# Down-projection passes with four seven-product pairs instead of two, and loads queued in unit order

## The chip, the cores and the metric

The kernel runs on one core of one Trainium2 chip. The metric is the device time of one execution in microseconds (us); lower is better. Several executions of each kernel are timed and their median is given, and one further execution is recorded by the hardware profiler. The engines are TensorE (PE, matrix products), VectorE (DVE), ScalarE (ACT), GpSimd (POOL) and SyncE (SP); the last issues most of the loads, and 16 DMA engines move the data.

## The reference, cut to what matters

One layer of a hybrid block on 256 tokens of width 2048, in float32: a normalised input projection, attention beside a convolution, an output projection, and then a SwiGLU feed-forward part of hidden width 5632. Only that last part is touched:

```python
hn = rms_norm(h, norm2_g[l])
a  = einsum('bsd,df->bsf', hn, w_gate[l])          # 256x2048 . 2048x5632
bu = einsum('bsd,df->bsf', hn, w_up[l])
h  = h + einsum('bsf,fd->bsd', silu(a) * bu, w_down[l])   # 256x5632 . 5632x2048
```

## The kernel before, in words

**Precision.** A float32 product is made of three matmuls in a reduced float32 format: each operand is split into a rounded part, "hi", and a residue, "lo", and hi·hi, lo·hi and hi·lo are added up in PSUM. So each weight tile that is loaded (`raw`, or `wb` for a pair) is rounded by ACT (`whi`, `wh`), and its residue (`wlo`, `wlt`, `wlb`) is found by a subtraction. The subtraction runs on DVE, or, where `by_dma` is set, ACT writes the negated raw tile and a DMA issued by POOL adds the raw tile to it (`round_chunk`, L320 to L324; the split on DVE is L329).

**The feed-forward part** works on hidden blocks of 512 columns. Blocks 0 to 10 lie in three groups of 4, 4 and 3 (`FGROUPS`). For each block, gate and up products are formed, multiplied and transposed (`transposed`, L831 to L842) into activations; after each group, `down_pass` multiplies the group's activations with the rows of `w_down` that belong to them. There are two passes for each group, each over 1024 output columns, in two halves of 512. A group of four blocks has 16 k-tiles of 128 rows; its two passes are called long passes here.

**Units.** The work is cut into units, listed in the order in which PE takes them (`ORDER`, `DORDERS`):

- A "two" (kind `g` or `u`, `multiply_two`) takes two k-tiles for one column half: 12 matmuls of 128x512. `g` is the first half and `u` the second.
- A "pair" (kind `s`, `multiply_pair`) takes two k-tiles for both column halves at once, by a scheme with seven products of block sums instead of eight: 21 matmuls, where four halves of twos would take 24. Its weights are combined by three operations on DVE (`round_pair`, L966 to L968), rounded by ACT (L969, L972) and split by DVE (`split_pair`, L975, L976). The activations need sums of their own, "forms", made by `make_down_forms` in small steps while the group's third and fourth blocks run.

In a long pass before the change, 2 of the 8 pairs of k-tiles go through pairs and the others through twos: the orders are `gguuggsguugsuu` and `sgggugggusuuuu`, 2 pairs and 12 twos each. All residues of these passes are found on DVE. A gate/up block has 4 pairs and 8 twos in the order `sggsggsuusuu`, and four of its twos have their residue made by DMA (two of them in the first block after a down pass).

**Order of the engines' queues.** No scheduler reorders anything: `run_chunks` writes out all instructions. When it is at unit t, it first writes the splits of units up to t+2, then loads, then the rounding of units up to t+3, and then unit t's matmuls. Each engine runs its own list in order and waits where a buffer or an operand isn't there yet. Loads of pairs are written six units ahead (`PAIR_AHEAD`), loads of twos three units ahead, at their rounding; both go through SP's queue, which stands still while its next load waits for a buffer. There are 5 buffers for `raw`, 2 for `wb`, 3 each for `whi` and `wlo`, 2 for `wh`, `wlt` and `wlb`, and 1 for `wt`. When the last unit with sums ends, `bank_sums` (L1092 to L1099) empties six PSUM banks, and `down_whole` (L1154) the other two; the next pass needs the same banks.

Of the kernel before, what the change touches and what calls it, by code (L numbers as in the profile page):

```python
# [12 lines left out]
F32 = mybir.dt.float32  # L13
F32R = mybir.dt.float32r
AF = mybir.ActivationFunctionType
# [70 lines left out]


HD = N // P
ND = 2
DORDERS = {4: ("gguuggsguugsuu", "sgggugggusuuuu"), 3: ("gguusggsuu", "gggsgsuuuu")}  # L90

Q1, Q6, Q7, Q5, Q2, Q4, Q3, QX = range(8)

# [2 lines left out]

HI_AHEAD, LO_AHEAD = 3, 2

PAIR_AHEAD = 6

FIRSTS = [sum(FGROUPS[: g + 1]) for g in range(len(FGROUPS))]

# [20 lines left out]
def tile_block(  # L123
# [117 lines left out]
    def start(gen):  # L241
        running.append(gen)
# [98 lines left out]
    def multiply(c):  # L341
# [42 lines left out]
        if c["done"]:  # L384
            start(c["done"](ps))

    def run_chunks():
        n = len(chunks)
        i = j = p = 0
        behind = [k for k in range(n) if chunks[k].get("kind") == "s"][NS]  # L390
        for t in range(n):
            hi_lead, lo_lead = lead(t)
            while j < min(i, t + 1 + lo_lead):
                chunks[j]["split"](chunks[j])
                j += 1
            while p < min(n, t + 1 + PAIR_AHEAD):
                if chunks[p].get("kind") == "s":

                    if p < behind and p > t + hi_lead:
                        break  # L400
                    load_pair(chunks[p])
                p += 1
            while i < min(n, t + 1 + hi_lead):
                if i in before:
                    before[i]()
                chunks[i]["load"](chunks[i])
                chunks[i]["round"](chunks[i])
# [413 lines left out]
    def transposed(j, aa):  # L821
        last = j + 1 in FIRSTS
        b = j - group_of(j)[1]
        for t in range(N // P // 2):

            pool_, tag = (acc_ps, "acc") if last else (aux_ps, "aux")
            pt = pool_.tile([P, 2, S], F32, tag=tag, name="ps_a")
            for i in range(2):
                for m in range(NM):
                    c = (2 * t + i) * P  # L830
                    pe.transpose(pt[:, i, m * P : (m + 1) * P], aa[m][:, c : c + P], ident)  # L831
# [10 lines left out]
            dve.tensor_tensor(lo, pt, hi.bitcast(F32), ALU.subtract)  # L842
# [14 lines left out]

    def make_down_forms(g):

        fp = ffn["pool"]  # L860
        gap = lambda: lag(5 if FGROUPS[g] == 4 else 2)
        a11, a21 = (raw_act[0][:, :, m * P : (m + 1) * P] for m in range(NM))
        a12, a22 = (raw_act[1][:, :, m * P : (m + 1) * P] for m in range(NM))

        hi = fp.tile([P, 7, ND, P], F32R, tag="dhi", name="dhi")
        lo = fp.tile([P, 3, ND, P], F32R, tag="dlo", name="dlo")
        fa, fb = (lhs.tile([P, 2, ND, P], F32, tag=t, name="dsums") for t in ("lhi", "llo"))
        act.copy(hi[:, 0], a11)
        dve.scalar_tensor_tensor(fa[:, 0], a21, -1.0, a22, ALU.mult, ALU.subtract)
        yield from gap()  # L870
        act.copy(hi[:, 1], a12)
        dve.scalar_tensor_tensor(fa[:, 1], fa[:, 0], -1.0, a11, ALU.mult, ALU.subtract)
        yield from gap()
        act.activation(hi[:, 2], a22, AF.Copy, scale=-1.0)
        dve.tensor_tensor(fb[:, 0], a11, a21, ALU.subtract)
        yield from gap()
        act.copy(hi[:, 3:5], fa)
        dve.tensor_tensor(fb[:, 1], a12, fa[:, 1], ALU.subtract)
        yield from gap()
        act.copy(hi[:, 5:7], fb)  # L880
        for i, a in ((0, a11), (1, a12)):
            dve.tensor_tensor(lo[:, i], a, hi[:, i].bitcast(F32), ALU.subtract)
            yield from gap()
        dve.scalar_tensor_tensor(lo[:, 2], a22, -1.0, hi[:, 2].bitcast(F32), ALU.mult, ALU.subtract)
        yield from gap()
        pairs = [lhs.tile([P, 2, ND, P], F32R, tag=t, name="dlo2") for t in ("lhi", "llo")]
        for i, f in ((0, fa), (1, fb)):
            dve.tensor_tensor(pairs[i], f, hi[:, 3 + 2 * i : 5 + 2 * i].bitcast(F32), ALU.subtract)
            yield from gap()
        los = [lo[:, 0], lo[:, 1], lo[:, 2], pairs[0][:, 0], pairs[0][:, 1], pairs[1][:, 0], pairs[1][:, 1]]  # L890
        down_forms[g] = {f: (hi[:, i], los[i]) for i, f in enumerate((0, 1, 3, 4, 5, 6, 2))}

    forms = {}
# [56 lines left out]
    def load_pair(c):  # L952
        c["b"] = early.tile([P, 4, N], F32, tag="wb", name="wb")
        for i, kind in enumerate("ug"):
            w, col = c["from"][kind]
            sp.dma_start(out=c["b"][:, 2 * i : 2 * i + 2, :],
                         in_=w.rearrange("(k p) n -> p k n", p=P)[:, c["rows"], col : col + N])
# [82 lines left out]
    def fast_block(order, pairs, twos, sources, operands, half, whole, by_dma=dict(g=(), u=())):  # L1040

        units, sums = [], {}
        left = dict(s=list(pairs), g=list(twos), u=list(twos))
        for kind in order:
            what = left[kind].pop(0)
            c = dict(kind=kind, sums=sums, done=None, first={}, last={}, rows=what["rows"], **operands)
            if kind == "s":
                c.update(p=what["p"], load=lambda c: None, round=round_pair, split=split_pair, multiply=multiply_pair,
                         uses=[q for q, _, _ in PRODUCTS])
# [12 lines left out]
        units[-1].update(done=whole, prompt=True)  # L1062
        chunks.extend(units)
# [8 lines left out]

    def down_pass(g, j0, nb):
        k0 = j0 * HD
        ks = [k for k in range(nb * HD) if k >= 2 * HD or k % HD >= ND]
        twos = [dict(ks=(k0 + a, k0 + b), rows=slice(k0 + a, k0 + b + 1, b - a), k=None)
                for a, b in zip(ks[::2], ks[1::2])]
        for i, order in enumerate(DORDERS[nb]):
            n = 2 * i
            end = {}  # L1080
            fast_block(order, [dict(p=p, rows=slice(k0 + p, k0 + p + HD + 1, HD)) for p in range(ND)], twos,
                       dict(g=(w_down, n * N), u=(w_down, (n + 1) * N)),
                       dict(pairs=lambda: down_forms.get(g), plain=actT.get),
                       lambda sums, n=n, end=end: down_half(g, n, sums, end),
                       lambda sums, n=n, end=end: down_whole(g, n, sums, end))

    halfway = {}

# [158 lines left out]
```

## Time and profile before

| | |
|---|---|
| Time, median of 3 runs | 1048.26 us (1048.14 to 1048.77) |
| Time of the profiled execution | 1048.92 us |
| Its span in the trace | 1047.1 us |
| PE busy | 1036.2 us, 4663 matmuls in the record |
| DVE busy | 900.6 us |
| ACT busy | 621.6 us |
| Clock granted to PE | full speed from the start |

A time in the profile is a time from the span's start. A matmul's recorded length overlaps the next one's, so the distance between starts tells what a matmul costs. "Idle before" in an engine's list is followed by what ended the wait. The long passes of the first group run from about 517 to 602 us, those of the second from about 769 to 854 us.

### The profile page before, as it was taken

To read this page: it belongs to the slowest core of one execution; us is meant where nothing else is said; L and a number is where in the kernel's file an instruction comes from. 1 tells how busy PE (TensorE), PEld (TensorE's weight loads), DVE (VectorE), ACT (ScalarE), POOL (GpSimd) and SP (SyncE) were. 2 spreads that over 40 slices of the span, in tenths; PEclk is the share of its full clock that TensorE was granted. 3 is DMA by queue.
4 is the path that set the end of the run, shared out by engine and by line. 5 is a ranking of instruction groups with operands and counts; after the bars stand their busy time and mean duration, and the time that the engine had idled before them with its cause. 6 is when DMAs were issued, how large, how long until landed. Compare 5 with 4: busy or idle time off the path is not lost.

```text
span 1047.1 us, 12933 instructions
## 1 busy us (share of the span) xinstructions
PE 1036.2 (99%) x4663; PEld 852.5 (81%) x4663; DVE 900.6 (86%) x1095; ACT 621.6 (59%) x786; POOL 100.5 (10%) x143
## 2 busy tenths in 40 slices
PE   9999999999999999999999999999999999999998
PEld 7888887877788788888888888888888888888886
DVE  7899889898765599999787898999878789989897
ACT  7544666755756565776463657666644446657442
POOL 0130122201100100000001010000000110000010
PEclk9999999999999999999999999999999999999999
DMA  9657654453546566987867789879757879798683
GB/s 335 227 182 280 212 163 167 154 181 134 177 153 226 194 223 214 268 266 236 232 210 188 217 271 273 256 217 285 248 175 241 219 208 291 222 287 267 187 265 85
DMA packets 113936, 231.30 MB, mean 221 GB/s; under 512 B 7504, under 2 KB 8656, under 8 KB 113616
## 3 DMA queue, kind: packets, MB, share of 16 engines
q1 hardware_dynamic: 104864, 203.71, 56.9%
q0 software_dynamic: 8864, 26.74, 13.4%
q8 instruction: 36, 0.59, 0.2%
q14 instruction: 28, 0.23, 0.1%
q10 hardware_dynamic: 144, 0.03, 0.0%
HBM read 204.24 MB, written 9.44 MB: 204 GB/s over the span
## 4 chain that ended last, share of the span: by engine, by line
PE 61%; DMA 2%; DVE 2%; issue 1%; ACT 0%; DVEq 0%; POOLq 0%
PE q L1020 12%; PE q L1014 12%; PE q L1015 12%; PE q L995 8%; PE q L993 7%; PE q L994 7%; DMA raw<-in_w_down_dram 1%; PE ps_a L831 1%; DMA wlo<-raw 1%; PE acc L365 1%; PE acc L359 1%; PE acc L360 1%; DVE wlo L329 1%; DVE wlt L976 0%; DVE wt L966 0%
## 5 line engine op out<-in xcount | busy, mean ns | idle before, releaser
L320 ACT CAST whi<-raw 128x1024 fp32r<-128x1024 f32 (+1 forms) x273 | 281.5, 1048 | 141.6 <-PE acc L360 58.9
L329 DVE TENSOR_TENSOR wlo<-raw,whi 128x1024 fp32r<-128x1024 f32 (+1 forms) x239 | 287.8, 1218 | 73.5 <-ACT whi L320 73.3
L972 ACT CAST wh<-wt 128x2048 fp32r<-128x2048 f32 x52 | 99.6, 1914 | 77.6 <-DVE wt L968 76.9
L976 DVE TENSOR_TENSOR wlt<-wt,wh 128x2048 fp32r<-128x2048 f32 x52 | 119.1, 2290 | 14.9 <-ACT wh L972 14.7
L359 PE MATMUL acc<-whi,xhi 128*128 128x512 f32 x320 | 126.9, 397 | 1.0 <-ACT whi L320 0.9
L360 PE MATMUL acc<-whi,xlo 128*128 128x512 f32 x320 | 125.2, 391 | 0.0
L1014 PE MATMUL q<-whi,chi 128*128 128x512 f32 x320 | 125.2, 391 | 0.0
L1015 PE MATMUL q<-whi,clo 128*128 128x512 f32 x320 | 124.5, 389 | 0.0
L993 PE MATMUL q<-wh,fhi 128*128 128x512 f32 x280 | 109.9, 393 | 0.0
L994 PE MATMUL q<-wh,flo 128*128 128x512 f32 x280 | 109.1, 390 | 0.0
L517 DVE SCALAR_TENSOR_TENSOR y<-upad,cw,y 128x256 f32<-128x256 f32 x240 | 102.2, 482 | 2.2 <-ACT y L510 2.2
L1014 PE MATMUL q<-whi,ahi 128*128 128x512 f32 x256 | 100.2, 391 | 0.0
L1015 PE MATMUL q<-whi,alo 128*128 128x512 f32 x256 | 99.6, 389 | 0.0
L975 DVE TENSOR_TENSOR wlb<-wb,wh 128x1536 fp32r<-128x1536 f32 x52 | 91.1, 1752 | 1.8 <-ACT wh L969 1.8
L365 PE MATMUL acc<-wlo,xhi 128*128 128x512 f32 x320 | 87.8, 396 | 2.0 <-DVE wlo L329 2.0
L1020 PE MATMUL q<-wlo,chi 128*128 128x512 f32 x320 | 85.7, 390 | 0.2 <-DMA wlo<-raw 0.2
L969 ACT CAST wh<-wb 128x1536 fp32r<-128x1536 f32 x52 | 76.6, 1474 | 0.0
L365 PEld LDWEIGHTS acc<-wlo,xhi 128*128 128x128 f32 x320 | 59.7, 189 | 15.3 <-DVE wlo L329 3.3
L359 PEld LDWEIGHTS acc<-whi,xhi 128*128 128x128 f32 x320 | 60.4, 189 | 14.3 <-ACT whi L320 1.9
L1020 PEld LDWEIGHTS q<-wlo,chi 128*128 128x128 f32 x320 | 59.9, 188 | 13.2 <-DMA wlo<-raw 0.8
L360 PEld LDWEIGHTS acc<-whi,xlo 128*128 128x128 f32 x320 | 60.4, 189 | 12.2
L1014 PEld LDWEIGHTS q<-whi,chi 128*128 128x128 f32 x320 | 60.1, 188 | 12.3
(230 smaller groups left out, 1739.1 us busy)
## 6 DMA issues: line engine op xcount, KB each, us to landing
raw<-in_w_in_dram SPq DMA_DIRECT2D x79, 512.0 KB, 4.6
raw<-in_w_down_dram SPq DMA_DIRECT2D x64, 512.0 KB, 7.2
raw<-in_w_gate_dram SPq DMA_DIRECT2D x48, 512.0 KB, 7.5
raw<-in_w_up_dram SPq DMA_DIRECT2D x48, 512.0 KB, 6.2
wb<-in_w_up_dram SPq DMA_DIRECT2D x40, 512.0 KB, 3.7
wb<-in_w_gate_dram SPq DMA_DIRECT2D x40, 512.0 KB, 4.9
wlo<-raw POOLq DMA_DIRECT2D x34, 512.0 KB, 7.1
raw<-in_w_out_dram SPq DMA_DIRECT2D x32, 512.0 KB, 4.2
```

Of the source, the lines that this page charges most:

```text
L320: act.copy(c["hi"], c["raw"])
L329: dve.tensor_tensor(c["lo"], c["raw"], c["hi"].bitcast(F32), ALU.subtract)
L359: pe.matmul(ps[m], xhi[:, ms], hi[:, j, :], start=c["first"] and j == 0, stop=False)
L360: pe.matmul(ps[m], xlo[:, ms], hi[:, j, :], start=False, stop=False)
L365: pe.matmul(ps[m], xhi[:, ms], lo[:, j, :], start=False, stop=c["last"] and j == nk - 1)
L517: dve.scalar_tensor_tensor(y[:, ct, :], src, wk, y[:, ct, :], ALU.mult, ALU.add)
L976: dve.tensor_tensor(lot, c["t"], c["hi"][:, :SUMMED].bitcast(F32), ALU.subtract)
L993: pe.matmul(ps, hi, c["hi"][:, w], start=bool(first), stop=False)
L994: pe.matmul(ps, lo, c["hi"][:, w], start=False, stop=False)
L1014: pe.matmul(ps, xs[i][0][:, ms], hi[:, i, :], start=i == 0 and bool(c["first"].get(qs[m])), stop=False)
L1015: pe.matmul(ps, xs[i][1][:, ms], hi[:, i, :], start=False, stop=False)
L1020: pe.matmul(sum_bank(c, qs[m]), xs[i][0][:, ms], lo[:, i, :], start=False, stop=i == 1 and bool(c["last"].get(qs[m])))
```

## The change

The long passes get 4 pairs and 8 twos each, in the orders `gguusgsgsusu` and `sggsggsuusuu`. Of the two blocks that feed the pairs, all four k-tiles are kept unsplit in one tile `raw_act`, and the forms are made over four k-tiles at once. In the first long pass of a group, the last two twos of either column half have their residue made by DMA; in the second, the second two of either half: six in a group's two passes. The short passes (last group) keep their orders. Loads of twos are now also written six units ahead, so that SP's queue holds all loads of these units in the order of the units; before, a pair's load stood ahead of those of the twos before it.

```diff
 HD = N // P
-ND = 2
-DORDERS = {4: ("gguuggsguugsuu", "sgggugggusuuuu"), 3: ("gguusggsuu", "gggsgsuuuu")}
+NDS = (4, 4, 2)
+DORDERS = {4: ("gguusgsgsusu", "sggsggsuusuu"), 3: ("gguusggsuu", "gggsgsuuuu")}
+DOWN_BY_DMA = {4: (dict(g=(2, 3), u=(2, 3)), dict(g=(1,), u=(1,))), 3: (dict(g=(), u=()),) * 2}
...
-PAIR_AHEAD = 6
+LOAD_AHEAD = 6
...
+    def load(c):
+        if not c.get("loaded"):
+            c["load"](c)
+            c["loaded"] = True
...
-            while p < min(n, t + 1 + PAIR_AHEAD):
-                if chunks[p].get("kind") == "s":
-
-                    if p < behind and p > t + hi_lead:
-                        break
-                    load_pair(chunks[p])
+            while p < min(n, t + 1 + LOAD_AHEAD):
+                kind = chunks[p].get("kind")
+                if kind and not (kind == "s" and p < behind and p > t + hi_lead):
+                    load(chunks[p])
                 p += 1
...
-                chunks[i]["load"](chunks[i])
+                load(chunks[i])
                 chunks[i]["round"](chunks[i])
...
-            if b < 2 and 2 * t < ND:
-                raw_act[b] = lhs.tile([P, 2, S], F32, tag=("lhi", "llo")[b], name=f"ar{j}")
-                act.copy(raw_act[b], pt)
+            g = group_of(j)[0]
+            nd = NDS[g]
+            if b < 2 and 2 * t < nd:
+                if not b and not t:
+                    raw_act[g] = ffn["pool"].tile([P, 2, nd, S], F32, tag="draw", name="raw_act")
+                act.copy(raw_act[g][:, b, 2 * t : 2 * t + 2, :], pt)
                 yield from lag(3 if last else 6)
-                if b:
-                    start(make_down_forms(group_of(j)[0]))
+                if b and 2 * t + 2 == nd:
+                    start(make_down_forms(g))
                 continue
...
     def make_down_forms(g):
...
+        hi = [one("lhi", F32R, "dhi") for _ in range(4)]
+        lo = [one("llo", F32R, "dlo") for _ in range(4)]
+        f4, f5, f6, f2 = (one(t, F32, "dsums") for t in ("lhi", "lhi", "llo", "llo"))
+        act.copy(hi[0], a11)
+        dve.scalar_tensor_tensor(f4, a21, -1.0, a22, ALU.mult, ALU.subtract)
...
+        hs = ffn["pool"].tile([P, 2, nd, P], F32R, tag="dhs", name="dhs")
+        for i, f in ((0, f4), (1, f5)):
+            act.copy(hs[:, i], f)
...
+        ls = ffn["pool"].tile([P, 4, nd, P], F32R, tag="draw", name="dls")
+        act.copy(ls[:, 3], f6)
+        for i, (f, h) in enumerate(((f4, hs[:, 0]), (f5, hs[:, 1]), (f6, ls[:, 3]))):
+            dve.tensor_tensor(ls[:, i], f, h.bitcast(F32), ALU.subtract)
+            if i:
+                yield from gap()
...
     def down_pass(g, j0, nb):
         k0 = j0 * HD
-        ks = [k for k in range(nb * HD) if k >= 2 * HD or k % HD >= ND]
-        twos = [dict(ks=(k0 + a, k0 + b), rows=slice(k0 + a, k0 + b + 1, b - a), k=None)
-                for a, b in zip(ks[::2], ks[1::2])]
+        nd = NDS[g]
+        ks = [k for k in range(nb * HD) if k >= 2 * HD or k % HD >= nd]
+        twos = [dict(ks=(k0 + a, k0 + b), rows=slice(k0 + a, k0 + b + 1, b - a), k=i)
+                for i, (a, b) in enumerate(zip(ks[::2], ks[1::2]))]
...
-                       lambda sums, n=n, end=end: down_whole(g, n, sums, end))
+                       lambda sums, n=n, end=end: down_whole(g, n, sums, end), DOWN_BY_DMA[nb][i])
```

Written out, the kernel has 24 matmuls less (6 for each of the four long passes), 8 pairs more and 16 twos less, 28 splits of twos less on DVE, and 12 residues by DMA more (46 instead of 34).

More of the change, by code (lines that the diff above doesn't have):

```diff
@@ L858, in make_down_forms @@
     def make_down_forms(g):
-        fp = ffn["pool"]
+        nd = NDS[g]
         gap = lambda: lag(5 if FGROUPS[g] == 4 else 2)
[L862 to L867, printed above, removed]
@@ L868, in make_down_forms @@
-        act.copy(hi[:, 0], a11)
-        dve.scalar_tensor_tensor(fa[:, 0], a21, -1.0, a22, ALU.mult, ALU.subtract)
+        raw = raw_act.pop(g)
+        a11, a21 = (raw[:, 0, :, m * P : (m + 1) * P] for m in range(NM))
+        a12, a22 = (raw[:, 1, :, m * P : (m + 1) * P] for m in range(NM))
+        one = lambda tag, dt, name: lhs.tile([P, 4, P], dt, tag=tag, name=name)[:, :nd]
+        hi = [one("lhi", F32R, "dhi") for _ in range(4)]
+        lo = [one("llo", F32R, "dlo") for _ in range(4)]
@@ L870, in make_down_forms @@
+        f4, f5, f6, f2 = (one(t, F32, "dsums") for t in ("lhi", "lhi", "llo", "llo"))
+        act.copy(hi[0], a11)
+        dve.scalar_tensor_tensor(f4, a21, -1.0, a22, ALU.mult, ALU.subtract)
         yield from gap()
-        act.copy(hi[:, 1], a12)
-        dve.scalar_tensor_tensor(fa[:, 1], fa[:, 0], -1.0, a11, ALU.mult, ALU.subtract)
+        act.copy(hi[1], a12)
+        dve.scalar_tensor_tensor(f5, f4, -1.0, a11, ALU.mult, ALU.subtract)
         yield from gap()
-        act.activation(hi[:, 2], a22, AF.Copy, scale=-1.0)
@@ L875, in make_down_forms @@
-        dve.tensor_tensor(fb[:, 0], a11, a21, ALU.subtract)
+        act.activation(hi[2], a22, AF.Copy, scale=-1.0)
+        dve.tensor_tensor(f6, a11, a21, ALU.subtract)
         yield from gap()
-        act.copy(hi[:, 3:5], fa)
-        dve.tensor_tensor(fb[:, 1], a12, fa[:, 1], ALU.subtract)
+        hs = ffn["pool"].tile([P, 2, nd, P], F32R, tag="dhs", name="dhs")
+        for i, f in ((0, f4), (1, f5)):
+            act.copy(hs[:, i], f)
+        dve.tensor_tensor(f2, a12, f5, ALU.subtract)
@@ L879, in make_down_forms @@
         yield from gap()
-        act.copy(hi[:, 5:7], fb)
+        act.copy(hi[3], f2)
         for i, a in ((0, a11), (1, a12)):
-            dve.tensor_tensor(lo[:, i], a, hi[:, i].bitcast(F32), ALU.subtract)
+            dve.tensor_tensor(lo[i], a, hi[i].bitcast(F32), ALU.subtract)
             yield from gap()
-        dve.scalar_tensor_tensor(lo[:, 2], a22, -1.0, hi[:, 2].bitcast(F32), ALU.mult, ALU.subtract)
+        dve.scalar_tensor_tensor(lo[2], a22, -1.0, hi[2].bitcast(F32), ALU.mult, ALU.subtract)
@@ L885, in make_down_forms @@
         yield from gap()
[L886 to L891, printed above, removed]
+        dve.tensor_tensor(lo[3], f2, hi[3].bitcast(F32), ALU.subtract)
@@ new lines, in make_down_forms @@
+        yield from gap()
[4 more added lines that the diff above has]
+            if i:
+                yield from gap()
+        down_forms[g] = {f: (hi[i], lo[i]) for i, f in enumerate((0, 1, 3, 2))}
+        down_forms[g].update({4: (hs[:, 0], ls[:, 0]), 5: (hs[:, 1], ls[:, 1]), 6: (ls[:, 3], ls[:, 2])})
@@ L1047, in fast_block @@
             if kind == "s":
-                c.update(p=what["p"], load=lambda c: None, round=round_pair, split=split_pair, multiply=multiply_pair,
+                c.update(p=what["p"], load=load_pair, round=round_pair, split=split_pair, multiply=multiply_pair,
                          uses=[q for q, _, _ in PRODUCTS])
@@ L1074, in down_pass @@
         k0 = j0 * HD
-        ks = [k for k in range(nb * HD) if k >= 2 * HD or k % HD >= ND]
-        twos = [dict(ks=(k0 + a, k0 + b), rows=slice(k0 + a, k0 + b + 1, b - a), k=None)
-                for a, b in zip(ks[::2], ks[1::2])]
+        nd = NDS[g]
+        ks = [k for k in range(nb * HD) if k >= 2 * HD or k % HD >= nd]
+        twos = [dict(ks=(k0 + a, k0 + b), rows=slice(k0 + a, k0 + b + 1, b - a), k=i)
+                for i, (a, b) in enumerate(zip(ks[::2], ks[1::2]))]
         for i, order in enumerate(DORDERS[nb]):
@@ L1080, in down_pass @@
             end = {}
-            fast_block(order, [dict(p=p, rows=slice(k0 + p, k0 + p + HD + 1, HD)) for p in range(ND)], twos,
+            fast_block(order, [dict(p=p, rows=slice(k0 + p, k0 + p + HD + 1, HD)) for p in range(nd)], twos,
                        dict(g=(w_down, n * N), u=(w_down, (n + 1) * N)),
```

## The prediction

> **What bounds the kernel now.** I read the page's busy times first, then the chain of waits through the long passes, then what PE waited for, the busy times by stage, and the order of the instructions on DVE, ACT and POOL in one gate/up block.
>
> ```profile
> PE 1036.2 (99%) x4663; PEld 852.5 (81%) x4663; DVE 900.6 (86%) x1095; ACT 621.6 (59%) x786; POOL 100.5 (10%) x143
> ```
>
> The chain at the start of a long pass shows what a matmul costs:
>
> ```profile
> 519.09 0.91 PE q L1020 x4
> 521.81 0.91 PE q L1020 x4
> 522.72 0.44 PE ps_a L831 x4
> ```
>
> From one two to the next is 521.81 − 519.09 = 2.72 us for 12 matmuls, so 0.2267 us each, with nothing between. Four transposes cost 0.44. What PE waited for from 380 us on, the whole of the part that the change touches (columns: total, times, longest):
>
> ```profile
> PE q L1020 <- DMA wlo<-raw: 0.2, 1, 0.2
> PE q L995 <- DVE wlt L976: 0.2, 1, 0.2
> ```
>
> So PE bounds this part, and a matmul taken out is worth its 0.2267 us until something else is late. How near the others are, by stage (the group's last gate/up block, its first and its second long pass; PE, PEld, DVE, ACT, POOL busy, clock, DMA share, GB/s):
>
> ```profile
> 475.50:517.30 41.80, 41.80 (x190) 34.61 (x189) 34.52 (x37) 24.74 (x25) 2.58 (x3) 1.00 0.80 233
> 517.30:560.40 43.10, 43.10 (x195) 35.49 (x195) 37.88 (x37) 23.42 (x22) 0.00 (x0) 1.00 0.63 208
> 560.40:602.60 42.20, 42.20 (x188) 34.95 (x187) 32.96 (x33) 19.74 (x18) 5.25 (x6) 1.00 0.78 204
> ```
>
> PE has no gap in any of them; DVE has about 5 to 9 us left in each.
>
> **What is removed.** Each long pass loses 4 twos (48 matmuls) and gains 2 pairs (42): 6 matmuls less. Four passes: 24 × 0.2267 = 5.44 us of PE. Everything below is what could give some of it back.
>
> **What a pair costs DVE and ACT.** One pair of block 3 on DVE (start, length; L842 and L888 are steps of other work):
>
> ```profile
> 487.46 1.22 DVE L329 TENSOR_TENSOR wlo<-raw,whi 128x1024 fp32r<-128x1024 f32 x1
> 488.60 1.22 DVE L966 TENSOR_TENSOR wt<-wb 128x1024 f32<-128x1024 f32 x1
> 489.85 0.69 DVE L967 TENSOR_TENSOR wt<-wb,wt 128x512 f32<-128x512 f32 x1
> 490.58 0.69 DVE L968 TENSOR_TENSOR wt<-wt,wb 128x512 f32<-128x512 f32 x1
> 491.19 0.69 DVE L842 TENSOR_TENSOR alo<-ps_a,ahi 128x512 fp32r<-128x512 f32 x1
> 491.79 1.75 DVE L975 TENSOR_TENSOR wlb<-wb,wh 128x1536 fp32r<-128x1536 f32 x1
> 493.45 2.29 DVE L976 TENSOR_TENSOR wlt<-wt,wh 128x2048 fp32r<-128x2048 f32 x1
> 495.65 0.69 DVE L888 TENSOR_TENSOR dlo<-dsums,dhi 128x512 fp32r<-128x512 f32 x1
> ```
>
> From start to start: the three combinations 2.59, `wlb` 1.66, `wlt` 2.20, so 6.45 for a pair; a two's split 1.14; a 512-wide step 0.60. PE takes 21 × 0.2267 = 4.76 for a pair and 2.72 for a two. A pair alone is thus slower on DVE than on PE, and it is the twos between pairs that pay for it. The same pair on ACT, and the residue that follows:
>
> ```profile
> 491.31 1.91 ACT L972 CAST wh<-wt 128x2048 fp32r<-128x2048 f32 x1 [1.34 <-DVE wt L968]
> 493.12 2.00 ACT L320 CAST whi<-raw 128x1024 fp32r<-128x1024 f32 x2
> 495.02 1.05 ACT L323 ACTIVATE wlo<-raw 128x1024 fp32r<-128x1024 f32 x1
> ```
>
> ```profile
> 436.97 0.87 POOL L324 DMA_DIRECT2D wlo<-raw  x1 [6.39 <-ACT wlo L323]
> ...
> 477.14 0.86 POOL L324 DMA_DIRECT2D wlo<-raw  x1 [6.13 <-DVE sum L1115]
> 496.43 0.86 POOL L324 DMA_DIRECT2D wlo<-raw  x1 [18.43 <-DVE dlo L888]
> ```
>
> ACT starts L972 as soon as L968 is done (490.58 + 0.69), and `wlt` can't start before L972 ends; with pairs back to back DVE's cycle is then 2.67 + 0.04 + 1.91 + 0.03 + 2.20 = 6.85. After L972, one rounding takes 0.95 to the next start, the negation 1.05, and POOL issues 0.36 later (496.43 − 496.07).
>
> **The first long pass after.** Its dense stretch is four times (pair, two), and all four twos have their residue by DMA. PE needs 7.48 for each, DVE 6.85, ACT 1.47 (estimate from the width: L969, 1536 against 2048 wide) + 1.91 + 1.05 + 1.05 = 5.5. So no engine is over, but each has little lead, and I follow them from the block's end as the profile of before has it:
>
> ```profile
> 517.99 1.28 DVE L1113 TENSOR_TENSOR sum<-q,sum 128x512 f32<-128x512 f32 x2
> 519.19 1.28 DVE L1115 TENSOR_TENSOR sum<-sum,sum 128x512 f32<-128x512 f32 x2
> 520.39 2.35 DVE L329 TENSOR_TENSOR wlo<-raw,whi 128x1024 fp32r<-128x1024 f32 x2
> ```
>
> PE starts the pass at 519.09 − 8 × 0.2267 = 517.28 and, unhindered, comes to the pairs s4, s6, s8, s10 (numbered by place) at 529.04, 536.52, 544.0, 551.48, and to the next pass at 558.96. DVE, in its new order: free at 520.39; one split 521.5, combinations 524.1, split 525.2, `wlb` 526.9, `wlt` of s4 done at 529.2, against 529.5 where PE first reads it. Then two steps of the last block's activations (0.60 each): `wlt` of s6 done 536.8 against 537.0; s8 543.7 against 544.5; s10 550.5 against 551.9. All in time, by 0.2 to 1.4.
>
> Residues: ACT ends L972 of s4 at 526.1, so POOL issues the first at about 528.4; PE reads it at 535.6, 7.2 later. For the second, L968 of s6 ends at 532.35, L972 at 534.3, POOL issues at 536.55, and PE reads it at 543.1 (541.28 for the two, and 8 matmuls): 6.55. The same working allows the third 6.9 and the fourth 7.6. What a residue takes from issue to landing (min, median, max of all 34, then the one issued at 477.14 alone):
>
> ```profile
> DMA to landing us min/median/max: 5.0/7.1/10.2
> ```
>
> ```profile
> DMA to landing us min/median/max: 5.0/5.0/5.0
> ```
>
> In the dense stretch each residue meets loads: the end of each `wlb` frees a `wb`, and three loads of 0.52 MB follow at once.
>
> ```profile
> q1 hardware_dynamic: 104864, 203.71, 56.9%
> q0 software_dynamic: 8864, 26.74, 13.4%
> ```
>
> By these rows (packets, MB, share of the 1047.1 us) a load is 0.524 × 0.569 × 1047.1 / 203.71 = 1.53 us of all DMA engines and a residue some 2.75, together 7.35 of each 7.48. So I take 8.0 for a landing, between the median and the longest. The first is then 0.8 late; the second, with PE already that much later, another 0.65; the third and the fourth not at all: 1.45. Here the Trainium skill would see no lateness: "DMA: Bandwidth & Descriptors", section on the anatomy of one DMA on the SWDGE path, fits 2.0 us plus the bytes over 436 GB/s, an estimate of 3.2 us for such a transfer. The trace's shortest is 5.0, so the trace decides; by the page only the next paragraph's lateness would stay.
>
> At the seam to the second long pass only one two (2.72) stands between the last sums and the next pair, where it was two twos; the sums of a block as they ran before:
>
> ```profile
> 510.51 0.59 ACT L1092 COPY sum<-q 128x512 f32<-128x512 f32 x1 [3.21 <-PE q L995]
> ```
>
> ```profile
> 511.13 0.69 DVE L1094 TENSOR_TENSOR sum<-q,sum 128x512 f32<-128x512 f32 x1 [2.57 <-ACT sum L1092]
> ...
> 513.93 0.68 DVE L1098 TENSOR_TENSOR sum<-q,sum 128x512 f32<-128x512 f32 x1
> ```
>
> ACT reaches the copy behind the roundings and the negation of the next pass's first two twos, at about 558.0, DVE starts the sums at 558.6, and the fifth, which frees the bank of the fourth product of the next pair, ends 3.5 later, at 562.1; PE wants it at 558.96 + 9 × 0.2267 = 561.0: 1.1 late. The same DVE list then gives the pass's second pair at 570.7 against 569.6, again 1.1. This runs beside the residues' lateness and isn't added to it: if PE is 1.45 late, both are in time. Behind that pair DVE gains again, because four twos and only two splits by DMA follow: its pass of 4 × 6.45 + 6 × 1.14 + 8 × 0.6 = 37.4 stands against PE's 40.8.
>
> **What I cost at nothing.** The forms are at most 11 steps of 0.69 for each group, 7.6, if nothing fell away for them; the last gate/up block's DVE has 41.80 − 34.52 = 7.3 free and the block before takes some. Without that cover they would cost up to 7.6 less what falls away. ACT's larger copies lie in stages where it is busy for 25 of 42. The loads in unit order give the twos' loads earlier; what SP stands still for now is mostly a free `wb`:
>
> ```profile
> SPq L956 <- DVE wlb L975: 336.4, 41, 13.4
> ```
>
> **Sum.** Profiled time 1048.92 − 5.44 + 2 × 1.45 = 1046.4; the median is 0.66 below the profiled execution, so 1048.26 − 5.44 + 2.9 = 1045.7. I call 0.2%, 2.1 us, what a measurement can tell from no change.
>
> **Rivals.** *All in time.* Residues land at the median or below where loads come early, and ACT and DVE keep a little more lead than my list: 1048.26 − 5.44 = 1042.8. For it: PE waited 0.4 in all with 34 residues, and loads in order could empty the DMA queues sooner. Against: nearly all of each 7.48 is filled with transfers.
>
> *Residues at their longest.* Each lands after 10.2: the second allows 6.55, so 3.65 late in each group, 1048.26 − 5.44 + 7.3 = 1050.1. It decides where landing is above 9.3, at which the gain is used up (2 × 2.72).
>
> *The new load order meets the gate/up blocks' residues (slower).* The second residue of a block is issued when SP stands still for a `wb`, and lands in 5.0. PE reads those of the first two POOL rows above at
>
> ```profile
> 443.55 0.91 PE q L1020 x4
> ...
> 485.28 0.91 PE q L1020 x4
> ```
>
> so it has 6.58 and 8.14. With more loads of twos queued ahead, SP can start one at just this time. At a landing of 8.65, midway between median and longest, these are 2.1 and 0.5 late; there are seven such blocks, so some 5 to 9 us, 7 in the middle: 1048.26 − 5.44 + 2.9 + 7 = 1052.7. It decides from a landing of about 7.5. The Trainium skill speaks for it: the same page, "Issuing engines are not separate DMA queues", says that all issuing engines' transfers interleave on the same 16 DMA engines; 5.0 in a quiet moment and 10.2 at the longest agree. Against: such a load is one, of 1.53, so 5.0 becomes about 6.5, under both allowances.
>
> **How the numbers follow.** Forecast 0.45 (own range 1043.5, a quarter of the lateness, to 1048.6, twice it); all in time 0.22; longest residues 0.15; load order 0.18. Faster by over 0.2% (below 1046.2): 0.22 and two thirds of the forecast, 0.52. Within 0.2%: the rest of the forecast, the longest residues and a little of the load order, 0.32. Slower: 0.16. The range, 1042.6 to 1050.6, takes in the first three and leaves out most of the fourth.
>
> **What would show it.** Right: 24 matmuls fewer, PE gaps of 1 to 2 us in each first long pass, released by `wlo<-raw`, or at the seam by DVE's sums; DVE at 37 to 40 of 41 in the passes. Wrong: no such gap (then 1042.8), gaps before L1020 of the gate/up blocks (the load order), waits for `wlt` in the third and fourth blocks (the forms), or for loads.

## The result, and the profile after

The changed kernel is slower: 1057.51 us (median of 6 runs, 1055.67 to 1059.56) against 1048.51 us (6 runs, 1048.14 to 1050.24); ratio 1.0083, 95% interval 1.0072 to 1.0093. The profiled execution took 1057.39 us, its span is 1055.6. The busy times of the page after:

```profile
PE 1033.1 (98%) x4639; PEld 848.3 (80%) x4639; DVE 924.1 (88%) x1109; ACT 645.8 (61%) x804; POOL 110.6 (10%) x155
```

The 24 matmuls are gone (4639 against 4663 in the record), and yet the span is 8.5 longer. What PE waited for after 380 us (columns: total, times, longest):

```profile
PE q L1034 <- DMA wlo<-raw: 4.0, 4, 1.5
PE q L1009 <- DVE wlt L990: 2.4, 2, 2.2
PE q L1007 <- DVE alo L849: 2.3, 2, 1.2
PE q L1034 <- DVE wlo L330: 1.8, 1, 1.8
PE acc L360 <- ACT whi L321: 0.9, 1, 0.9
```

Before, this list held 0.4 us. The timeline of PE says where these waits lie. Three stand together where block 0 ends and block 1 begins, the first block that has pairs; the diff names neither block:

```profile
388.97 0.50 PE L360 MATMUL acc<-whi,hhi 128*128 128x512 f32 x1 [0.87 <-ACT whi L321]
395.65 1.20 PE L1034 MATMUL q<-wlo,chi 128*128 128x512 f32 x4 [1.85 <-DVE wlo L330]
399.52 0.50 PE L1009 MATMUL q<-wlt,fhi 128*128 128x512 f32 x1 [2.22 <-DVE wlt L990]
...
401.34 0.63 PE L1009 MATMUL q<-wlt,fhi 128*128 128x512 f32 x1
401.76 0.63 PE L1007 MATMUL q<-wh,fhi 128*128 128x512 f32 x1
```

The others are the same three in each first long pass (those of the first group):

```profile
539.28 0.50 PE L1007 MATMUL q<-wh,dhi 128*128 128x512 f32 x1 [1.16 <-DVE alo L849]
544.90 1.20 PE L1034 MATMUL q<-wlo,ahi 128*128 128x512 f32 x4 [1.48 <-DMA wlo<-raw]
553.39 1.20 PE L1034 MATMUL q<-wlo,ahi 128*128 128x512 f32 x4 [0.69 <-DMA wlo<-raw]
```

The first transposes that PE does in a block (of the activations of the block before) are good milestones, because every kernel has them. Their starts on PE (some records are missing, so a start is good to about 0.2):

| first transpose in block | before | after | shift |
|---|---|---|---|
| 1 | 396.74 | 403.04 | +6.3 |
| 2 | 438.36 | 444.61 | +6.25 |
| 3 | 480.12 | 486.37 | +6.25 |
| 5, behind the first group's passes | 648.16 | 655.76 | +7.6 |
| 7 | 731.75 | 739.26 | +7.5 |
| 9, behind the second group's passes | 899.81 | 908.30 | +8.5 |

So 6.3 us are lost before any changed pass begins, and each group's passes grow by 1.35 and 0.98 where 2.72 should have fallen away. No gate/up block but block 1 loses anything. Of the two passes of a group, only the first one loses. The second one begins and ends with these matmuls, before and after:

```profile
560.34 0.39 PE L993 MATMUL q<-wh,dhi 128*128 128x512 f32 x1
602.50 0.39 PE L993 MATMUL q<-wh,fhi 128*128 128x512 f32 x1
```

```profile
569.39 0.39 PE L1007 MATMUL q<-wh,dhs 128*128 128x512 f32 x1
610.19 0.39 PE L1007 MATMUL q<-wh,fhi 128*128 128x512 f32 x1
```

That is 42.16 before and 40.80 after, 1.36 less, which is just the 6 × 0.2267 that a pass was to save; the second group has the same two lengths.

Block 1's loss starts in SP's queue. Before (start, length, engine, line; the first row groups eight loads, issued within 20.19):

```profile
352.16 20.19 SPq L315 DMA_DIRECT2D raw<-in_w_up_dram  x8
377.44 0.37 SPq L956 DMA_DIRECT2D wb<-in_w_up_dram  x1
377.85 0.46 SPq L956 DMA_DIRECT2D wb<-in_w_gate_dram  x1
```

After:

```profile
371.71 0.37 SPq L316 DMA_DIRECT2D raw<-in_w_gate_dram  x1
375.31 0.37 SPq L316 DMA_DIRECT2D raw<-in_w_up_dram  x1
380.15 0.37 SPq L316 DMA_DIRECT2D raw<-in_w_gate_dram  x1
384.16 0.37 SPq L316 DMA_DIRECT2D raw<-in_w_up_dram  x1
384.58 0.46 SPq L970 DMA_DIRECT2D wb<-in_w_up_dram  x1
385.09 0.46 SPq L970 DMA_DIRECT2D wb<-in_w_gate_dram  x1
```

The units of block 0 have no `kind`, so the new rule leaves their loads at their rounding, while the twos of block 1 are loaded six units ahead. These take the `raw` buffers first; block 0's last `w_up` load goes out at 384.16 instead of about 372, and the first pair's load stands behind it, 7.2 later than before (385.09 against 377.85). The chain of waits goes on from this load (start, length, what):

```profile
385.09 6.60 DMA wb<-in_w_gate_dram
...
391.78 1.24 DVE wt L980
```

### The profile page after: what moved, and what is told of

It is laid out like the page before. It is cut to its first block, busy times and chain, and to the rows that moved or that the text cites. A ratio compares the mean times of both kernels' runs of the same rounds, so it can differ in the third digit from the quotient of the medians.

```text
span 1055.6 us, 12970 instructions
## 1 busy us (share of the span) xinstructions
PE 1033.1 (98%) x4639; PEld 848.3 (80%) x4639; DVE 924.1 (88%) x1109; ACT 645.8 (61%) x804; POOL 110.6 (10%) x155
## 4 chain that ended last, share of the span: by engine, by line
PE 56%; DMA 3%; issue 3%; DVE 2%; ACT 0%; SPq 0%; DVEq 0%; POOL 0%; POOLq 0%; ACTq 0%
PE q L1034 10%; PE q L1028 10%; PE q L1029 10%; PE q L1009 8%; PE q L1007 8%; PE q L1008 8%; DMA wlo<-raw 2%; DMA raw<-in_w_down_dram 1%; PE ps_a L835 1%; DVE wlo L330 1%; DMA wb<-in_w_gate_dram 1%; DVE wlt L990 0%; PE acc L366 0%; PE acc L360 0%; PE acc L361 0%
## 5 line engine op out<-in xcount | busy, mean ns | idle before, releaser
L321 ACT CAST whi<-raw 128x1024 fp32r<-128x1024 f32 (+1 forms) x257 | 264.7, 1047 | 100.0 <-PE acc L361 55.0
L330 DVE TENSOR_TENSOR wlo<-raw,whi 128x1024 fp32r<-128x1024 f32 (+1 forms) x211 | 254.4, 1216 | 52.9 <-ACT whi L321 52.7
L986 ACT CAST wh<-wt 128x2048 fp32r<-128x2048 f32 x60 | 114.9, 1914 | 99.8 <-DVE wt L982 99.6
L990 DVE TENSOR_TENSOR wlt<-wt,wh 128x2048 fp32r<-128x2048 f32 x60 | 137.4, 2290 | 18.9 <-ACT wh L986 18.8
L989 DVE TENSOR_TENSOR wlb<-wb,wh 128x1536 fp32r<-128x1536 f32 x60 | 105.0, 1751 | 1.0 <-ACT wh L983 1.0
L983 ACT CAST wh<-wb 128x1536 fp32r<-128x1536 f32 x60 | 88.5, 1475 | 11.5 <-PE q L1008 6.7
L325 POOL DMA_DIRECT2D wlo<-raw x46 | 39.7, 863 | 517.2 <-ACT wlo L324 308.9
L980 DVE TENSOR_TENSOR wt<-wb 128x1024 f32<-128x1024 f32 x60 | 73.1, 1218 | 5.8 <-DMA wb<-in_w_gate_dram 3.1
L1028 PE MATMUL q<-whi,ahi 128*128 128x512 f32 x192 | 75.3, 392 | 0.0
L1029 PE MATMUL q<-whi,alo 128*128 128x512 f32 x192 | 74.8, 389 | 0.0
```

Source lines behind the costliest of these rows:

```text
L321: act.copy(c["hi"], c["raw"])
L330: dve.tensor_tensor(c["lo"], c["raw"], c["hi"].bitcast(F32), ALU.subtract)
L986: act.copy(c["hi"][:, :SUMMED], c["t"])
L990: dve.tensor_tensor(lot, c["t"], c["hi"][:, :SUMMED].bitcast(F32), ALU.subtract)
L1028: pe.matmul(ps, xs[i][0][:, ms], hi[:, i, :], start=i == 0 and bool(c["first"].get(qs[m])), stop=False)
L1029: pe.matmul(ps, xs[i][1][:, ms], hi[:, i, :], start=False, stop=False)
```

## The experiments

My theory when I began: the load order costs 6.3 us, all in block 1; the first long passes lose theirs to late residues and to a PSUM bank, and their own saving is real. Each kernel was timed beside the kernel before on the same chip, whose medians there were 1048.73 to 1048.96.

**1. The order alone.** The kernel before with the new load rule.

```diff
...
-                if chunks[p].get("kind") == "s":
-
-                    if p < behind and p > t + hi_lead:
-                        break
-                    load_pair(chunks[p])
+                kind = chunks[p].get("kind")
+                if kind and not (kind == "s" and p < behind and p > t + hi_lead):
+                    load(chunks[p])
```

> The kernel before with only the new order of loads. Theory: the 6.3 us that the changed kernel loses where block 1 begins come from this order alone (three loads of block 1's twos hold raw buffers that block 0's last w_up loads need, and the first pair's load stands behind them): 1048.5 + 6.3 = 1054.8, with PE waits for wlt and wlo near 390 to 400 us. Rival: the order is harmless, and that loss comes from the other parts of the change: 1048.5.

Measured: 1054.98 us, ratio 1.0057 (1.0042 to 1.0072). The waits after 380 us are block 1's three and nothing else:

```profile
PE q L998 <- DVE wlt L979: 2.4, 2, 2.2
PE q L1023 <- DVE wlo L329: 1.7, 1, 1.7
PE acc L359 <- ACT whi L320: 0.9, 1, 0.9
```

The order by itself costs 6.3 us, at that one place.

**2. The passes without the order.** The changed kernel with the load rule of before.

```diff
-                kind = chunks[p].get("kind")
-                if kind and not (kind == "s" and p < behind and p > t + hi_lead):
+                if chunks[p].get("kind") == "s":
+                    if p < behind and p > t + hi_lead:
+                        break
                     load(chunks[p])
```

> The changed kernel with the old order of loads everywhere. Theory: the loss at block 1 is gone and the one in the first long passes (about 4 us in each group) stays: 1057.5 - 6.3 = 1051.2. Rival: the loads in order also crowd the residues in the passes; then their landing falls to about 8 us here and the passes lose 1 to 1.5 us each: about 1045 to 1046.

Measured: 1092.2 us, ratio 1.0420 (1.0400 to 1.0441). Both expectations were far off. In a first long pass a pair's load now stands ahead of the `raw` load of the two that precedes it, and waits for a free `wb`. SP (timeline):

```profile
527.41 0.47 SPq L316 DMA_DIRECT2D raw<-in_w_down_dram  x1
540.98 0.92 SPq L971 DMA_DIRECT2D wb<-in_w_down_dram  x2
541.95 0.46 SPq L316 DMA_DIRECT2D raw<-in_w_down_dram  x1
553.22 0.91 SPq L971 DMA_DIRECT2D wb<-in_w_down_dram  x2
```

SP stands still for 11 to 13 us at a time, the residues come late, and the pairs behind them free their buffers later still: a ring of waits. PE's list has 15.6 us for `wlo<-raw` and 14.0 for `alo`. At this lead of six units the new pass order can't do without the load order, which costs 6 us in block 1 and saves 41 in the passes.

**3. The order from the second block of pairs on.**

```diff
+        ordered = behind
...
-                if kind and not (kind == "s" and p < behind and p > t + hi_lead):
+                if kind == "s" and p < behind and p > t + hi_lead:
+                    break
+                if kind == "s" or kind and t >= ordered:
```

> The changed kernel with loads in unit order only from the second block of pairs on, the old order before. Theory: nothing is lost at block 1, and everything behind it is as in the changed kernel, first-pass waits for wlo, for a bank freed by alo and all: 1051.2. Rival (the loss at block 1 has another cause, such as a longer start of the pairs): stays at 1057.

Measured: 1051.48 us, ratio 1.0033 (1.0019 to 1.0047), as the theory has it: 6 us are back, and block 1's waits are gone:

```profile
PE q L1037 <- DMA wlo<-raw: 4.1, 6, 1.4
PE q L1010 <- DVE alo L852: 2.4, 2, 1.2
```

What is left are the waits of the first long passes, and the change without block 1's loss is still slower than the kernel before. The experiments that follow start from this kernel and look at these passes.

**4. No residue by DMA in the long passes.**

```diff
-DOWN_BY_DMA = {4: (dict(g=(2, 3), u=(2, 3)), dict(g=(1,), u=(1,))), 3: (dict(g=(), u=()),) * 2}
+DOWN_BY_DMA = {4: (dict(g=(), u=()),) * 2, 3: (dict(g=(), u=()),) * 2}
```

> As the one before, and all residues of the long passes on DVE instead of six in a group by DMA. Theory: no wait for wlo from a DMA in the passes (2 us gained in each), but DVE's cycle for a pair and a two is 6.85 + 1.14 = 8.0 against PE's 7.48, so that PE waits for wlt by about 0.5 for each of four pairs and at the seam: within 2 us of the one before, 1049 to 1053. Rival (the residues are innocent, DVE alone sets the first passes): slower than the one before by the whole 12 x 1.14 = 13.7 us of added splits or a large part of it, 1056 and more.

Measured: 1059.54 us, ratio 1.0102 (1.0087 to 1.0117). I had expected too little: this is the time of the rival (1056 and more). DVE's cycle is the reckoned 8.0 (`wlt` starts at 544.19, 552.19, 560.19), and its lateness shows up at every operand of its own:

```profile
PE q L1010 <- DVE alo L852: 4.7, 2, 2.3
PE q L1012 <- DVE wlt L993: 3.2, 5, 0.9
PE q L1010 <- DVE sum L1116: 2.1, 2, 1.0
```

The DMA residues are late but worth 8 us: DVE is the other bound of these passes.

**5 to 7. The two latenesses, one at a time and together.** 5 rounds every unit of the first long passes (marked `dense`) one unit earlier; 6 puts the second `alo` step ahead of the next pair's combinations; 7 does both.

```diff
...
+                    c["dense"] = True
...
-    lead = lambda t: (1, 1) if t < OPENING else (HI_AHEAD, LO_AHEAD) if near_pair(t) else (AHEAD, AHEAD)
+    lead = lambda t: (1, 1) if t < OPENING else (4, LO_AHEAD) if chunks[t].get("dense") else (HI_AHEAD, LO_AHEAD) if near_pair(t) else (AHEAD, AHEAD)
```

```diff
-            yield from lag(1 if last else 2)
+            yield from lag(0 if last and t and NDS[group_of(j)[0]] == 4 else 1 if last else 2)
```

> The kernel with the order from block 2 on (1051.5), and in the first long passes twos and pairs are rounded four units ahead instead of three, so that a residue's DMA is issued some 4 us earlier (before the rounding of the pair ahead of it). Theory (the residues' late landing costs about 2.1 us in each first pass, the wait for a bank held by alo 1.4): no wait for wlo from DMA left, 1051.5 - 4.2 = 1047.3. Rival (landing only stretches by what is gained, since the DMA engines are full, or the seam's late sums take over): 1050 to 1051.5.

> The same kernel at 1051.5, and only the last alo step of a long pass is put ahead of the next pair's combinations on DVE. Theory (of several latenesses in a row only the last to end counts): the wait for the bank, 1.2 us a pass, goes, and the wait for the first residue grows by as much: 1051.5, no change within 0.7. Rival (each wait adds up by itself): 1051.5 - 2.7 = 1048.8.

> Both of the two steps before. Theory: neither wait is left and what remains is the seam between the passes (DVE's sums and the next pair, 1.1 us by the lists): 1051.5 - 7.3 + 2.2 = 1046.4, faster than before by 0.2%. Rival (the stalls come back in another wait of the same size): 1049 or more.

Measured: 1054.9 us, ratio 1.0055 (1.0038 to 1.0072); 1054.61, 1.0058 (1.0043 to 1.0073); 1055.41, 1.0067 (1.0045 to 1.0089). None gains. In 5 the waits for residues are gone, but the pair that is rounded earlier puts its combinations ahead of `alo`, whose wait grows to 2.1, and the seam appears:

```profile
PE q L1010 <- DVE alo L852: 4.2, 2, 2.1
PE q L1010 <- DVE sum L1119: 2.1, 2, 1.0
```

These are the waits of an execution of 1052.12 with a mean granted clock of 1.000; the other three took 1054.05 to 1056.15 with a clock of 0.996 to 0.998. So most of what 5 loses against experiment 3 is not in these waits.

In 6 the wait for `alo` is gone and the first residue's has taken it in, in one piece:

```profile
541.19 2.07 PE L1037 MATMUL q<-wlo,ahi 128*128 128x512 f32 x4 [3.31 <-DMA wlo<-raw]
543.06 0.63 PE L1010 MATMUL q<-wh,dhs 128*128 128x512 f32 x1
543.49 0.63 PE L1011 MATMUL q<-wh,dls 128*128 128x512 f32 x1
```

Lateness that lies in one queue is not a sum of waits: what ends first only uncovers what ends next. In waits, 6 is what I expected, 3.31 against 1.21 + 1.40 + 0.37 in experiment 3. In time it is not: from block 3 to block 5 it takes 171.56 against 168.98, because the matmuls behind the gap are 0.43 apart instead of 0.227 until 546.9 (the mean clock is 0.94 between 516 and 570). In 7 `alo` still waits 2.08, behind which the clock is 0.79 between 532 and 540.

**8. Fewer loads beside the residues.** In each first long pass three of the four pairs use the first one's weights and load none.

```diff
...
+        if "like" in c:
+            c["b"] = c["like"]["b"]
+            return
...
+                for c in pairs[1:]:
+                    c["like"] = pairs[0]
```

> The kernel at 1051.5 with the pair loads of the first long passes left out behind the first one (the three other pairs of such a pass use the first pair's weights, so its products are other ones). Theory (a residue lands late because it shares the DMA engines with the loads that the end of each wlb sets off): the four residues of a pass land after 5 to 7.5 us instead of 10.1, 10.1, 8.6 and 7.9, no wait for wlo from DMA is left, 1047.3. Rival (the landing is long for another reason, such as the order in the POOL queue or the transfer's own work): landing and waits as before, 1051.

Measured: 1052.42 us, ratio 1.0030 (1.0017 to 1.0043): not what I expected of the sum, but the durations are what the run was for. The first three residues of the first group's pass, set off at the same distances as in experiment 3, land after 6.1, 4.5 and 4.6 us, where experiment 3 has 10.1, 10.1 and 8.6. The fourth meets the loads of the next pass, which SP now issues from 549.23 on, takes 11.0, and PE waits for it:

```profile
551.88 0.86 POOL L325 DMA_DIRECT2D wlo<-raw  x1 [6.26 <-ACT wlo L324]
```

```profile
562.91 1.20 PE L1040 MATMUL q<-wlo,ahi 128*128 128x512 f32 x4 [2.31 <-DMA wlo<-raw]
```

So about half of a residue's time among the loads is due to them. What was left to try is to set it off earlier, and without moving DVE's list, which 5 had done.

**9. The kernel before with the order from block 2 on.** Experiment 3's rule, the old passes.

> The kernel before with the new load order alone, and that only from the second block of pairs on. Theory (the order costs 6.3 us in the first block of pairs and nothing in the blocks and passes behind it): 1048.5, and every transposed tile of the later blocks stands where it stands in the kernel before, within 0.3 us. Rival (the order also changes what the long passes cost, so a part of the two groups' losses is the order's and not the pass order's): another time than 1048.5 by over 1 us, with the difference between block 3 and block 5.

Measured: 1049.79 us, ratio 1.0008 (0.9998 to 1.0017). From block 3 to block 5 it is 649.59 − 481.46 = 168.13, against 168.04; from 7 to 9 168.06 against 168.06. The passes don't feel the order, as the theory says. The blocks do, against it (it had every transposed tile within 0.3): the 1 us lies between blocks 1 and 3, where the switch makes a residue 0.5 late twice:

```profile
422.84 1.20 PE L1025 MATMUL q<-wlo,chi 128*128 128x512 f32 x4 [0.55 <-DMA wlo<-raw]
444.55 1.21 PE L1025 MATMUL q<-wlo,chi 128*128 128x512 f32 x4 [0.52 <-DMA wlo<-raw]
```

**10. The twos alone rounded earlier, with `alo` ahead.** Experiment 6's kernel, with the twos of places 5, 7, 9 and 11 of a first long pass marked `dense`.

```diff
...
+            if i == t + 4 < n and chunks[i].get("dense"):
+                load(chunks[i])
+                chunks[i]["round"](chunks[i])
+                chunks[i]["rounded"] = True
...
+                for k in (5, 7, 9, 11):
+                    chunks[k - len(order)]["dense"] = True
```

> The changed kernel with the order from the second block on, the second step of the last tile's rounding ahead of the next pair's combinations, and in the first long passes the four twos among the pairs rounded one unit earlier than the pairs are, so that their residues are set off before ScalarE waits for the pair's combinations. Theory (the two latenesses of a first long pass are the residues and the bank that the last block's tile holds; with both gone the passes keep what they save, less the seam's wait for the sums of about 1.4 a group that showed where the residues were in time): residues set off 2.5 to 5 us earlier than with the order alone, no wait for wlo or alo over 0.3, 1043.1 + 2.8 + 0.6 for slower first matmuls behind gaps = 1046.5, between 1045.5 and 1048. Rival (the transfers set off earlier only land later, because they share the engines with the same loads): the waits for wlo stay, 1050 or more.

Measured: 1047.91 us, ratio 0.9990 (0.9981 to 0.9999). The residues are set off at 524.85, 531.27, 539.21 and 546.62, 4.3 to 6.0 earlier than in experiment 3, and land after 4.8, 7.6, 7.2 and 9.6: the rival, that they would only land later, is out. In the long passes only the seam is left (1.03), and 0.26 for `wlt`; outside them residues are late by 0.26, 0.49 and, in block 5, 0.80.

**11. The seam.** As 10, with the second pass's residue by DMA for its first two instead of its second, rounded early as well.

```diff
-DOWN_BY_DMA = {4: (dict(g=(2, 3), u=(2, 3)), dict(g=(1,), u=(1,))), 3: (dict(g=(), u=()),) * 2}
+DOWN_BY_DMA = {4: (dict(g=(2, 3), u=(2, 3)), dict(g=(0,), u=(1,))), 3: (dict(g=(), u=()),) * 2}
...
+                chunks[1 - len(order)]["dense"] = True
```

> As the one before, and in the second long pass the residue by DMA is taken for the first two instead of the second, and this two is rounded early as well, so that no residue of VectorE's stands ahead of the sums at the seam. Theory (the seam's wait is the 1.2 us residue ahead of the sums in VectorE's queue): the waits for the sums fall from 0.4 + 1.0 to under 0.4 a group, 1044.5, between 1043.5 and 1046.5, faster than the kernel before by 0.2 to 0.5 per cent. Rival (the seam waits for ScalarE's copy of the first bank or for the residue that now comes by DMA, needed 5 us earlier): a wait of over 1 us stays at the seam or in the unit behind it, 1046 to 1048.

Measured: 1049.3 us, ratio 1.0003 (0.9995 to 1.0012). My theory falls. The split is out of the way, but ACT, which serves the early two before the pair's `wh`, waits for the pair's load first (timeline of ACT, then of DVE):

```profile
552.21 1.48 ACT L991 CAST wh<-wb 128x1536 fp32r<-128x1536 f32 x1 [2.75 <-DMA wb<-in_w_down_dram]
...
555.50 1.90 ACT L994 CAST wh<-wt 128x2048 fp32r<-128x2048 f32 x1
```

```profile
557.43 2.29 DVE L998 TENSOR_TENSOR wlt<-wt,wh 128x2048 fp32r<-128x2048 f32 x1 [0.85 <-ACT wh L994]
559.64 0.68 DVE L1122 TENSOR_TENSOR sum<-q,sum 128x512 f32<-128x512 f32 x1
```

So `wlt` ends late and the sums start at 559.64 instead of 559.89 in experiment 10, not 1.2 earlier; the wait at the seam stays 0.97, and the split that now stands behind the sums makes the next pair's `wlt` 0.87 late. This is the rival's picture.

**12. The order in the long passes only.** As 10, but the units of the long passes alone are loaded in order, and what lies ahead of the first of them is loaded first.

```diff
-                if kind == "s" or kind and t >= ordered:
+                if chunks[p].get("ordered"):
+                    for k in range(i, p):
+                        load(chunks[k])
+                if kind == "s" or chunks[p].get("ordered"):
...
+                for c in chunks[-len(order):]:
+                    c["ordered"] = True
```

> The version with the twos rounded early, but loads are queued in order in the long passes of the first two groups alone; where such a pass begins, the units ahead of it that are not loaded yet are loaded first, and the gate/up blocks keep the load rule of the kernel before. Theory (the switch to the new order in block 2 costs 0.6 to 0.7 us once, and a residue that came 0.8 late in block 5 is the order's too; the long passes alone need the order): the blocks take what they take in the kernel before, each group stays 0.9 shorter than there, so 1.8 us less than the kernel before, 1047.0 where that one takes 1048.8, between 1046.3 and 1047.9. Rival (each start of a long pass pays for the switch again, in wb or raw loads that come late): a wait of 0.5 us or more at the start of each of the two groups' passes, 1048 or more.

Measured: 1047.67 us (11 runs, 1046.57 to 1048.65), ratio 0.9988 (0.9979 to 0.9997), span 1045.0. The expected 1047.0 is 0.7 off, the range holds it. PE's waits after 380 us:

```profile
PE q L1017 <- DVE sum L1129: 2.0, 2, 1.0
PE q L1019 <- DVE wlt L1000: 0.7, 3, 0.3
PE q L1044 <- DMA wlo<-raw: 0.3, 1, 0.3
```

The transposes in block 5 stand at 646.90 (before 648.16), those in block 9 at 897.69 (before 899.81); 0.4 of this already stands at block 1, ahead of any changed pass. This version is clearly faster than the changed kernel. Against the kernel before, 0.12% is less than the 0.2% that I said one measurement can tell; the interval just leaves 1 out, so that it is faster is likely and not more.

## Why the prediction was wrong, step by step

- **Removed work: right.** 24 matmuls are gone from the record, and the second long pass of either group is shorter by the whole 1.36 already in the changed kernel (40.80 against 42.16). The first one has it eaten up by its waits.
- **VectorE's and ScalarE's timetable: right.** With PE 6.24 later by block 1's loss, the first two residues were to be issued at 534.65 and 542.8; the trace has

```profile
534.65 0.89 POOL L325 DMA_DIRECT2D wlo<-raw  x1 [21.65 <-ACT wlo L324]
542.83 0.86 POOL L325 DMA_DIRECT2D wlo<-raw  x1 [7.29 <-ACT wlo L324]
```

- **The landing of a residue: mis-sized.** I took 8.0. They took 10.2, 10.5, 9.4 and 8.0, so the first two waited 1.48 and 0.69 behind a PE that was already 1.16 late; without that, experiment 6 shows 3.31. Here the longest value of before was the right one, not one between it and the median: the row of the whole trace mixed quiet and crowded places, and I had worked out that this place was the most crowded. The Trainium skill's fit ("DMA: Bandwidth & Descriptors", anatomy of one DMA on the SWDGE path: 3.2 us as an estimate for this size) is not reached even with the pairs' loads taken away (4.5 in experiment 8).
- **The bank of the last block's tile: missed.** I followed operands of the first pair and not its results. Its fifth product (PE waits at 539.28, behind 12 matmuls of the pair) takes the last of four `acc` banks, in which the last block's transposed tile stood until the second `alo` step, and that step stands behind the next pair's combinations in DVE's list: 1.16 and 1.17 in the two groups.
- **The seam: right,** 1.1 predicted and hidden as long as PE is late elsewhere; 1.03 where it isn't (10 and 12).
- **"What I cost at nothing": half wrong, and this is the step that failed most.** The forms cost nothing, as said: from block 2 to block 3 it is 41.76 in both kernels. The loads in unit order cost 6.3 us (experiment 1). The prediction put them at nothing because SP stands still mostly for a free `wb`. That looks at what SP's queue waits for as a total, and not at the place where the new rule meets units that it doesn't cover.
- **The rival of the load order** had the right culprit and the wrong place. It made residues of seven gate/up blocks late; none of these blocks lost anything, and all of the loss stood at the border to block 0. So its sum of 1052.7, though nearer, was right by no step of it. Nor does its price follow from its own figures: 2.1 late in each of seven blocks would be 14.7, not 5 to 9.
- **The rival of the longest residues** had the landing right (10.2, against 10.2 and 10.5) and came near a group's lateness by residues alone (3.65, against 3.31 in experiment 6). It knew neither the bank nor block 1's 6.3, which its 1050.1 lacks.
- **The sum.** −5.44, +6.3 for block 1, and +4.07 and +3.70 for the passes (1.35 and 0.98 longer, plus 2.72 each) make +8.6, against 8.5 in the span. I had +2.9 for both groups and nothing for block 1. Of the first group's 4.07, listed waits are 1.16 + 1.48 + 0.69 = 3.33. The rest is how a wait is listed: it counts from the recorded end of the matmul before, 0.39 after its start, where the next one could have started after 0.227; and the matmul behind a gap is 0.34 from the next. So a gap costs some 0.16 + 0.11 = 0.27 more than its row, three gaps 0.8, and 4.1 is all of the 4.07. The same working on experiment 12 gives 0.25 + 1.02 + 2 × 0.27 = 1.8 for the first group, which leaves 0.9 of 2.72; from block 3 to block 5 it saves 0.89.

## What to carry to other kernels

A rule that loads some kinds of units earlier must be followed at its border, where these loads meet units that keep the old rule and share their buffers; a total of a queue's waits doesn't show that. Where a schedule is late at several operands of one engine's queue, list all of them (results' banks too) and take them off together, because taking one off uncovers the next. For a transfer whose time differs twofold between quiet and crowded places, take the duration from the place most like the one it is going to.

## What the runs showed that I had not expected

A wait of PE can cost more than its length. Behind block 1's gaps of 1.85 and 2.22 us, which end 3.9 us apart, some six matmuls are 0.43 apart (0.227 elsewhere), and the granted clock of the stretch is 0.96 (columns as in the stages of before: PE, PEld, DVE, ACT and POOL busy, clock, DMA share, GB/s):

```profile
398.20:440.00 41.80, 40.48 (x175) 33.42 (x176) 38.51 (x35) 24.60 (x23) 2.65 (x3) 0.96 0.79 239
```

It happened behind single gaps of 3.31 (experiment 6) and 2.08 (experiment 7), and not behind 2.31 and 2.65 (experiment 8, clock 1.00). Even the same gap can do either: experiment 4 waits 2.35 for `alo` in both first long passes, and the clock behind it is 1.00 in the first group (534 to 545) and 0.84 in the second (791 to 802). Executions of one kernel differ by it too: experiment 3 took 1051.03 to 1051.48 with a mean clock of 1.000 and 1053.74 to 1053.84 with 0.998. What decides it stays open. The Trainium skill ("TensorE: Matmul & The Clock Gate", section on HAM oscillation) says that a gap of PE over some 3.4 us sends the clock to half. Half agrees with 0.43; the length doesn't: these gaps are all shorter, and they aren't sorted by length either.

The same accumulating transfer of a 128x1024 tile takes 4.5 to 6.1 us where few loads run beside it and 7 to 11 us among the loads of pairs, and the loads that are left out in one stretch come earlier in the next and lengthen it there (experiment 8).
